# A two-block layer on one core: the depthwise convolution's work divided anew between VectorE, TensorE and an accumulating DMA

## The chip, the cores and the metric

The kernel runs on one core of a Trainium2 chip. The metric is the device time of one execution in microseconds (us), as the median of several runs.

## What is computed

The reference runs two model blocks on 256 tokens of width 1024, all in float32: a first block (a gated feed-forward, a token mixer with two kinds of attention, another feed-forward) and a second block (a Conformer convolution, a feed-forward, a gate, attention with forget gates, and so on). The change lies in the convolution of the second block:

```python
def conformer_conv(hn, w_pw1, b_pw1, w_dw, b_dw, ln_g, ln_b, w_pw2, b_pw2):
    u = hn @ w_pw1 + b_pw1
    a, g = jnp.split(u, 2, axis=-1)
    u = a * jax.nn.sigmoid(g)
    kern = w_dw[:, None, :].astype(u.dtype)
    u = lax.conv_general_dilated(
        u, kern, window_strides=(1,), padding=((CONV_WIDTH - 1, 0),),
        dimension_numbers=("NWC", "WIO", "NWC"),
        feature_group_count=D_MODEL) + b_dw
    u = layernorm(u, ln_g, ln_b)
    u = jax.nn.silu(u)
    return u @ w_pw2 + b_pw2
```

Each of the 1024 channels is filtered by its own 31 taps over the 256 tokens, causally. Before it stands a product with a 1024x2048 matrix, behind it a layer norm over the channels, which needs every channel.

## The kernel before

**The weight stream.** Activations lie transposed, 128 channels on the partitions and 256 tokens along the free dimension; 1024 channels are eight such tiles. All weights come as one stream of chunks of 128x1024 float32 (512 KB, eight 128x128 blocks). SP loads a chunk into a `raw` buffer (5 of them). ScalarE copies it into `hi`, rounded to fp32r (L239, 4 buffers), and VectorE writes the rest, raw minus hi, into `lo` (L243, 4 buffers). A product of a block with an activation, which is split in the same way, is then three fp32r matmuls (`mm3`, L260 to L262: hi with the activation's upper part, hi with its lower part, lo with its upper part).

**The convolution's stage** (`conv`, L1159). For each of the eight channel tiles n, `pw1(n)` makes two groups of 24 such matmuls, one for each half of the gate, from one chunk each, so the stage uses 16 chunks. VectorE multiplies each half by the row scale R (L1186, L1189), ScalarE adds biases and takes a tanh, VectorE joins both into `cu`, the padded input of the filter (L1193). ScalarE copies `cu` into `cx`, which holds even and odd tokens apart (L1199, four small copies).

`conv_out(n)` filters one tile. The 31 taps are divided: TensorE takes LAGS = 11 pairs of taps in each of two groups g of 64 channels, as float32 matmuls with diagonal matrices `cw` or `dw` (L1214; one float32 matmul is two rows of the trace). ScalarE brings the two results into `cb` (L1217). VectorE takes the other REST = 10 taps as shifted products, one instruction a tap, in two chains of five (tile `a` for even, tile `t` for odd taps): the first of a chain is a TENSOR_SCALAR (L1226), the others SCALAR_TENSOR_TENSORs that add to the chain (L1228). Then it adds the two chains (L1229), for n > 0 a `shift` (L1231), and in `stats` the TensorE part `cb` (L1236). The shift, tile `cm`, is tile 0's mean over its channels, negated, taken from the finished tile 0 by a matmul (L1240) and a copy (L1242); it goes to every tile so that the later variance is well behaved. `stats` also sums the tiles and their squares (L1250, L390) for the layer norm.

**What sets the order.** The program is written with tiles and pools, and a scheduler orders the instructions of each engine ahead of time, by its own estimate of when each can run. On the chip each engine then takes its instructions strictly in that order, and a waiting instruction holds up everything behind it on its engine.

```python
            for d in range(LAGS):
                nc.tensor.matmul(o, w[:, d], x[:, g, 16 - d : 16 + P - d], start=(d == 0), stop=(d == LAGS - 1))
```

Of the kernel before, what the change touches and what calls it, by code (L numbers as in the profile page):

```python
# [9 lines left out]
F32 = mybir.dt.float32  # L10
# [3 lines left out]
ALU = mybir.AluOpType  # L14
# [11 lines left out]
EPS = 1e-6  # L26
NEG = -1e30
TAPS = 31
LAGS = 11
AHEAD = 2  # L30
WARM = 10
WIDE = 6
# [84 lines left out]
class Kern:  # L117
# [104 lines left out]
    def prefetch(self, two=False):  # L222
# [17 lines left out]

        def low(i):
            s = slice(i * h, (i + 1) * h)
            nc.vector.tensor_tensor(lo[:, s], raw[:, s], hi[:, s].bitcast(F32), op=ALU.subtract)  # L243

        self.ready.append((chunk, hi, lo))
# [913 lines left out]
    def conv(self, X, R, after):  # L1159
# [44 lines left out]
        def conv_out(n, u, x):  # L1204
            b = self.bank("pt")
            back = self.p([P, T], "cb", 2)
            for g in range(2):
# [7 lines left out]
                for r in range(2):  # L1215
# [2 lines left out]
                        back[g * HD : g * HD + HD, r::2], o[h], AF.Identity, scale=0.5, bias=dwb[h, n, g : g + 1]  # L1218
                    )

            v = [self.a("u"), self.t("t")]
            for i in range(REST):
                w = v[i % 2]
                s, c = u[:, i : i + T], dww[:, n, i : i + 1]
                if i < 2:
                    nc.vector.tensor_scalar(w, s, c, None, op0=ALU.mult)  # L1226
                else:
                    nc.vector.scalar_tensor_tensor(w, s, c, w, op0=ALU.mult, op1=ALU.add)  # L1228
            nc.vector.tensor_tensor(v[0], v[0], v[1], op=ALU.add)  # L1229
            if n:  # L1230
                nc.vector.tensor_tensor(v[0], v[0], self.shift, op=ALU.add)  # L1231
            return v[0], back

        def stats(n, v, back):
            nonlocal acc, acc2
            nc.vector.tensor_tensor(v, v, back, op=ALU.add)  # L1236
            if n == 0:

                b = self.bank("pt")
                nc.tensor.matmul(b[:, :T], nmean, v, start=True, stop=True)  # L1240
                self.shift = self.p([P, T], "cm0", 1)
                nc.vector.tensor_copy(self.shift, b[:, :T])  # L1242
                v0 = v
                v = self.a("v")
                nc.vector.tensor_tensor(v, v0, self.shift, op=ALU.add)
                acc = self.t("acc")
                nc.vector.tensor_copy(acc, v)
            else:
                if n < KD - 1:
                    nc.vector.tensor_tensor(acc, acc, v, op=ALU.add)  # L1250
            acc2 = self.square_into(acc2, v, n == KD - 1)
            U.append(v)

        todo = []
        for n in range(KD):
            x = pw1(n)
            if n > 1:
                stats(n - 2, *todo.pop(0))
            if n:
                todo.append(conv_out(n - 1, *prev))  # L1260
            prev = x
        todo.append(conv_out(KD - 1, *prev))
        for n in (KD - 2, KD - 1):
            stats(n, *todo.pop(0))
        self.stage = "convLN"
        XP = [self.split(t) for t in self.ple_loads(0)]
        while len(self.ready) < PRE:
# [495 lines left out]
```

## Time and profile before

| | |
|---|---|
| median of three runs | 1367.5 us (1366.8, 1367.5, 1372.15) |
| profiled execution, its own time | 1364.68 us |
| its span | 1362.9 us |
| TensorE (PE) busy | 1337.7 us, 98% of the span |
| VectorE (DVE) busy | 1066.6 us, 78% |
| ScalarE (ACT) busy | 860.0 us, 63% |
| GpSimd (POOL) busy | 146.8 us, 11% |
| DMA | 234.11 MB, mean 172 GB/s |

The span is the profiler's stretch from the first to the last instruction; the execution's own time holds 1.8 us more around it. A busy share is an average over stages with different limits: what a change in one stage is worth is read from that stage, from the time of each engine in it and from the wait that ends last there. Matmuls overlap in the records, so what one costs is the distance between the starts of neighbours, not its duration. The same holds for neighbours on the other engines.

### The profile page before, as it was taken

The page shows a single profiled execution, that of the slowest core. Times are in us where ns is not written, and L with a number is a line of the kernel's source. Part 1 is how long each engine was busy: PE and PEld are TensorE (multiplying, and loading weights), DVE is VectorE, ACT ScalarE, POOL GpSimd, SP SyncE. Part 2 cuts the span into 40 slices and gives each one's busy share as a digit, 9 for nine tenths or more (in the row PEclk, how much of TensorE's full clock was granted, in tenths as well). Part 3 has the DMA queues.
Part 4 walks back from the last instruction along what each step waited for, and adds up shares of the span by engine and source line. Part 5 has one row for each costly group of instructions (what it writes and reads, how often), then busy time and mean ns, then how long its engine had stood idle before and what let it go on. Part 6 is the DMA issues. An engine that isn't in the chain of part 4 may idle for free. (4 is left out here: it accounts for less than half of the span.)

```text
span 1362.9 us, 25065 instructions
## 1 busy us (share of the span) xinstructions
PE 1337.7 (98%) x9111; PEld 1210.0 (89%) x9111; DVE 1066.6 (78%) x2381; ACT 860.0 (63%) x1994; POOL 146.8 (11%) x197
## 2 busy tenths in 40 slices
PE   8999999999999999999999999999999999999997
PEld 7888898899988998888899998888897989888887
DVE  7877668798887779987779798766678986976665
ACT  6666544678787556666655586654557785665554
POOL 0111000000000001310010003220001210431000
PEclk9999999999999999999999999999999999999999
DMA  8666665643332655666666145666655444666561
GB/s 281 186 186 186 189 190 201 232 128 121 110 109 84 193 175 185 189 198 186 193 220 226 73 139 183 194 194 188 189 168 163 140 124 140 202 189 193 189 188 45
DMA packets 65228, 234.11 MB, mean 172 GB/s; under 512 B 7536, under 2 KB 8208, under 8 KB 65104
## 3 DMA queue, kind: packets, MB, share of 16 engines
q1 hardware_dynamic: 63648, 230.89, 54.0%
q8 instruction: 72, 1.18, 0.3%
q10 hardware_dynamic: 1296, 1.35, 0.3%
q0 software_dynamic: 160, 0.26, 0.1%
q14 instruction: 52, 0.43, 0.1%
HBM read 231.43 MB, written 1.05 MB: 171 GB/s over the span
## 5 line engine op out<-in xcount | busy, mean ns | idle before, releaser
L239 ACT ACTIVATE hi<-raw 128x512 fp32r<-128x512 f32 (+1 forms) x759 | 471.9, 666 | 382.7 <-issue 187.8
L243 DVE TENSOR_TENSOR lo<-raw,hi 128x512 fp32r<-128x512 f32 (+1 forms) x759 | 542.9, 749 | 180.3 <-ACT hi L239 178.1
L260 PE MATMUL mm<-a,hi 128*128 128x256 f32 x654 | 194.2, 297 | 0.5 <-ACT a L1127 0.5
L262 PE MATMUL mm<-a,lo 128*128 128x256 f32 x654 | 185.0, 283 | 0.0
L261 PE MATMUL mm<-a,hi 128*128 128x256 f32 x654 | 184.9, 283 | 0.0
L271 PE MATMUL at<-a,hi 128*128 128x512 f32 x408 | 146.9, 398 | 2.3 <-DVE a L368 2.3
L271 PE MATMUL s<-a,hi 128*128 128x512 f32 x416 | 148.2, 394 | 0.0
L271 PE MATMUL mm<-a,hi 128*128 128x512 f32 x392 | 139.8, 394 | 0.0
L365 POOL TENSOR_TENSOR H<-t,H 128x256 fp32r<-128x256 f32 x108 | 105.9, 981 | 302.5 <-ACT H L364 298.3
L260 PEld LDWEIGHTS mm<-a,hi 128*128 128x128 f32 x654 | 125.2, 191 | 4.2 <-issue 2.7
L261 PEld LDWEIGHTS mm<-a,hi 128*128 128x128 f32 x654 | 125.2, 191 | 0.0
L262 PEld LDWEIGHTS mm<-a,lo 128*128 128x128 f32 x654 | 124.8, 191 | 0.0
L272 PE MATMUL s<-a,lo 128*128 128x256 f32 x416 | 116.5, 280 | 0.0
L272 PE MATMUL at<-a,lo 128*128 128x256 f32 x408 | 115.1, 282 | 0.5 <-DVE lo L243 0.5
L271 PE MATMUL at<-H,hi 128*128 128x512 f32 x324 | 113.0, 393 | 0.0
L272 PE MATMUL mm<-a,lo 128*128 128x256 f32 x392 | 109.8, 280 | 0.0
L271 PE MATMUL mm<-H,hi 128*128 128x512 f32 x292 | 102.0, 393 | 0.0
L271 PEld LDWEIGHTS at<-a,hi 128*128 128x128 f32 x408 | 77.1, 189 | 20.2 <-ACT hi L239 2.6
L271 PEld LDWEIGHTS s<-a,hi 128*128 128x128 f32 x416 | 78.0, 187 | 17.7
L272 PE MATMUL at<-H,lo 128*128 128x256 f32 x324 | 90.1, 278 | 0.0
L271 PEld LDWEIGHTS mm<-a,hi 128*128 128x128 f32 x392 | 73.5, 187 | 16.5
L271 PE MATMUL s<-H,hi 128*128 128x512 f32 x248 | 86.4, 393 | 0.0
(412 smaller groups left out, 2980.3 us busy)
## 6 DMA issues: line engine op xcount, KB each, us to landing
raw<-in_wts SPq DMA_DIRECT2D x423, 512.0 KB, 4.2
cw<-in_dwp SPq DMA_DIRECT2D x9, 704.0 KB, 4.6
x<-in_xT SPq DMA_DIRECT2D x4, 256.0 KB, 6.2
raw<-in_wts SPq DMA_DIRECT2D x2, 256.0 KB, 5.8
e<-in_pT ACTq DMA_DIRECT2D x4, 128.0 KB, 5.1
out_dram<-o ACTq DMA_DIRECT2D x2, 256.0 KB, 3.0
out_dram<-o SPq DMA_DIRECT2D x2, 256.0 KB, 3.1
cst<-in_cst SPq DMA_DIRECT2D x1, 416.0 KB, 8.2
```

The source lines that it names most:

```text
L239: nc.scalar.activation(hi[:, s], raw[:, s], AF.Copy)
L243: nc.vector.tensor_tensor(lo[:, s], raw[:, s], hi[:, s].bitcast(F32), op=ALU.subtract)
L260: nc.tensor.matmul(out, sh, mh, start=(first and i == 0), stop=False)
L261: nc.tensor.matmul(out, sh, ml, start=False, stop=False)
L262: nc.tensor.matmul(out, sl, mh, start=False, stop=(last and i == n - 1))
L271: nc.tensor.matmul(b, sh, m.rearrange("p i n -> p (i n)"), start=(k == 0), stop=False)
L272: nc.tensor.matmul(b[:, T:], sl, mh, start=False, stop=(k == len(X) - 1))
L365: (low or nc.vector).tensor_tensor(lo, src, hi.bitcast(F32), op=ALU.subtract)
```

## The change

Three things are done, all in the convolution's stage.

1. The 16 chunks that are loaded for `pw1` get their `lo` in another way. ScalarE writes `lo` = -`hi`, and a DMA issued by GpSimd then reads the chunk from HBM a second time and adds it to `lo` in place. VectorE's subtraction is gone for these chunks.
2. LAGS goes from 11 to 9, so REST goes from 10 to 14: TensorE loses two lags in each of the 16 groups, VectorE gains four taps in each of the eight tiles. The tables `cw` and `dw` shrink from 11 to 9 matrices.
3. Two additions are folded into the chains: the even chain begins with a SCALAR_TENSOR_TENSOR that adds `shift` (for n > 0), the odd chain with one that adds `cb`. The additions of L1231 and L1236 are gone.

```diff
-LAGS = 11
+LAGS = 9
@@ prefetch
         def low(i):
             s = slice(i * h, (i + 1) * h)
+            if self.stage == "conv":
+
+                nc.scalar.mul(lo[:, s], hi[:, s].bitcast(F32), -1.0)
+                nc.gpsimd.dma_start(lo[:, s], self.ap["wts"][chunk, :, s], accum_op=ALU.add)
+                return
             nc.vector.tensor_tensor(lo[:, s], raw[:, s], hi[:, s].bitcast(F32), op=ALU.subtract)
@@ conv_out
             v = [self.a("u"), self.t("t")]
+            base = [self.shift if n else None, back]
             for i in range(REST):
                 w = v[i % 2]
                 s, c = u[:, i : i + T], dww[:, n, i : i + 1]
-                if i < 2:
+                on = base[i] if i < 2 else w
+                if on is None:
                     nc.vector.tensor_scalar(w, s, c, None, op0=ALU.mult)
                 else:
-                    nc.vector.scalar_tensor_tensor(w, s, c, w, op0=ALU.mult, op1=ALU.add)
+                    nc.vector.scalar_tensor_tensor(w, s, c, on, op0=ALU.mult, op1=ALU.add)
             nc.vector.tensor_tensor(v[0], v[0], v[1], op=ALU.add)
-            if n:
-                nc.vector.tensor_tensor(v[0], v[0], self.shift, op=ALU.add)
-            return v[0], back
+            return v[0]
 
-        def stats(n, v, back):
+        def stats(n, v):
             nonlocal acc, acc2
-            nc.vector.tensor_tensor(v, v, back, op=ALU.add)
```

The new lines push the later line numbers up by five to seven. The scheduler makes a new order of everything in the stage. Three places of it matter here. The numbers in the names tell buffers apart.

**GpSimd's queue at the start of the stage, before.** `dww` and `dwb` are the tap weights of VectorE and the biases, `rs_y` are two reciprocal roots from which the row scale R is made:

```order
L1171 DMA dww_8781<-in_dww 128x80
L1174 DMA dwb_8784<-in_dwb 128x16
L1192 MEMSET cu_8856 128x30
L1196 MEMSET cx_8859 128x2x16
L1192 MEMSET cu_8933 128x30
L1196 MEMSET cx_8936 128x2x16
L1192 MEMSET cu_9055 128x30
L1192 MEMSET cu_9188 128x30
L407 TENSOR_TENSOR rs_y_8733<-rs_v_8731,mhalf 128x2
L407 TENSOR_TENSOR rs_y_8741<-rs_v_8739,mhalf 128x2
```

The same place now; `lo_8903` is the last of four accumulating loads that stand ahead, `lo_8996` the first of twelve that follow:

```order
L246 DMA lo_8903<-in_wts 128x1024
L1176 DMA dww_8781<-in_dww 128x112
L1179 DMA dwb_8784<-in_dwb 128x16
L1197 MEMSET cu_8858 128x30
L1201 MEMSET cx_8861 128x2x16
L1197 MEMSET cu_8937 128x30
L1201 MEMSET cx_8940 128x2x16
L1197 MEMSET cu_9061 128x30
L1197 MEMSET cu_9194 128x30
L412 TENSOR_TENSOR rs_y_8733<-rs_v_8731,mhalf 128x2
L412 TENSOR_TENSOR rs_y_8741<-rs_v_8739,mhalf 128x2
L246 DMA lo_8996<-in_wts 128x1024
```

So `dww` stands behind four accumulating loads, and the fifth such load stands behind both roots.

**TensorE at the fifth chunk of the stage, before** (`s`, `mm` and `at` are PSUM banks; `hi_8991` and `lo_8992` are the fifth chunk, `hi_9021` the sixth):

```order
L262 MATMUL s_8866<-a_8717,lo_8900 128x256
L260 MATMUL mm_8987<-a_8134,hi_8991 128x256
L261 MATMUL mm_8987<-a_8134,hi_8991 128x256
L260 MATMUL at_8988<-a_8134,hi_9021 128x256
L261 MATMUL at_8988<-a_8134,hi_9021 128x256
L262 MATMUL mm_8987<-a_8134,lo_8992 128x256
```

And now, where `hi_8995`, `hi_9026`, `hi_9128` and `hi_9159` are the fifth to the eighth chunk:

```order
L267 MATMUL s_8868<-a_8717,lo_8903 128x256
L265 MATMUL mm_8991<-a_8134,hi_8995 128x256
L266 MATMUL mm_8991<-a_8134,hi_8995 128x256
L265 MATMUL at_8992<-a_8134,hi_9026 128x256
L266 MATMUL at_8992<-a_8134,hi_9026 128x256
L265 MATMUL s_9124<-a_8134,hi_9128 128x256
L266 MATMUL s_9124<-a_8134,hi_9128 128x256
L265 MATMUL mm_9125<-a_8134,hi_9159 128x256
L266 MATMUL mm_9125<-a_8134,hi_9159 128x256
L267 MATMUL mm_8991<-a_8134,lo_8996 128x256
```

TensorE begins four chunks ahead, with the products that need `hi` alone, before the first that needs the fifth chunk's `lo`.

**VectorE at the end of the stage, before.** These are the last instructions ahead of the layer norm's column sums; `cb_9749` is the TensorE part of the last tile, n = 7, and `cb_9707` that of n = 6:

```order
L1229 TENSOR_TENSOR a_9734<-a_9734,t_9735 128x256
L390 TENSOR_TENSOR acc_9073<-acc_9073,sq_9580 128x256
L1229 TENSOR_TENSOR a_9734<-a_9734,t_9776 128x256
L1250 TENSOR_TENSOR acc_9071<-acc_9071,a_9487 128x256
L1231 TENSOR_TENSOR a_9734<-a_9734,cm_9067 128x256
L390 TENSOR_TENSOR acc_9073<-acc_9073,sq_9703 128x256
L1231 TENSOR_TENSOR a_9734<-a_9734,cm_9067 128x256
L1236 TENSOR_TENSOR a_9734<-a_9734,cb_9707 128x256
L1250 TENSOR_TENSOR acc_9071<-acc_9071,a_9734 128x256
L390 TENSOR_TENSOR acc_9073<-acc_9073,sq_9791 128x256
L1236 TENSOR_TENSOR a_9734<-a_9734,cb_9749 128x256
```

And now, from the instruction that takes the last tile's `cb` in, with `t_9736` and `t_9776` the odd chains of n = 6 and n = 7:

```order
L1236 SCALAR_TENSOR_TENSOR t_9776<-cu_9698,dww_8781,cb_9753 128x256
L395 TENSOR_TENSOR acc_9078<-acc_9078,sq_9708 128x256
L1236 SCALAR_TENSOR_TENSOR t_9736<-cu_9575,dww_8781,t_9736 128x256
L1236 SCALAR_TENSOR_TENSOR a_9735<-cu_9698,dww_8781,a_9735 128x256
L1236 SCALAR_TENSOR_TENSOR t_9776<-cu_9698,dww_8781,t_9776 128x256
L1236 SCALAR_TENSOR_TENSOR t_9736<-cu_9575,dww_8781,t_9736 128x256
L1236 SCALAR_TENSOR_TENSOR t_9776<-cu_9698,dww_8781,t_9776 128x256
L1236 SCALAR_TENSOR_TENSOR t_9736<-cu_9575,dww_8781,t_9736 128x256
L1236 SCALAR_TENSOR_TENSOR t_9776<-cu_9698,dww_8781,t_9776 128x256
L1237 TENSOR_TENSOR a_9735<-a_9735,t_9736 128x256
L1236 SCALAR_TENSOR_TENSOR t_9776<-cu_9698,dww_8781,t_9776 128x256
L1255 TENSOR_TENSOR acc_9076<-acc_9076,a_9735 128x256
```

Behind the last row shown stand two more steps of `t_9776`, a sum of squares and the joining addition. `cb` of a tile was the last thing that VectorE added; now it goes into the first of the odd chain's seven steps, and the other six and an addition follow it.

## Rows read from the trace of the kernel before

**Rows 1.** Windows view: busy us of each engine, TensorE clock, DMA share, GB/s
```profile
core 0: us, PE busy (x) PEld busy (x) DVE busy (x) ACT busy (x) POOL busy (x), PEclk, DMA share, GB/s
690.00:760.00 70.00, 68.93 (x586) 68.52 (x585) 62.19 (x152) 38.80 (x80) 4.89 (x18) 1.00 0.68 230
760.00:780.00 20.00, 20.00 (x180) 20.00 (x179) 15.19 (x43) 12.48 (x35) 0.25 (x2) 1.00 0.01 2
784.00:786.00 2.00, 2.00 (x11) 2.00 (x11) 1.15 (x7) 0.38 (x1) 0.69 (x1) 0.50 0.00 0
786.00:788.00 2.00, 2.00 (x14) 2.00 (x13) 1.04 (x3) 0.38 (x1) 0.00 (x0) 0.66 0.00 0
```
**Rows 2.** Timeline of TensorE: start, us, instruction, count, [idle before it, releaser]
```profile
691.30 0.28 PE L260 MATMUL mm<-a,hi 128*128 128x256 f32 x1
...
697.19 0.29 PE L261 MATMUL s<-a,hi 128*128 128x256 f32 x1
...
715.47 0.28 PE L261 MATMUL at<-a,hi 128*128 128x256 f32 x1
715.59 2.62 PE L1214 MATMUL pt<-cx,cw 128*128 128x128 f32 x22
717.96 0.36 PE L262 MATMUL at<-a,lo 128*128 128x256 f32 x1
...
756.10 5.18 PE L1214 MATMUL pt<-cx,cw 128*128 128x128 f32 x44 [1.07 <-ACT cb L1217]
...
780.47 0.28 PE L398 MATMUL pt<-ones,acc 128*128 128x1 f32 x2
```
**Rows 3.** Timeline of VectorE in the convolution's stage, the same columns
```profile
699.69 0.20 DVE L1172 TENSOR_SCALAR dww<-dww 128x80 f32<-128x80 f32 x1 [3.51 <-DMA dww<-in_dww]
...
704.41 2.35 DVE L243 TENSOR_TENSOR lo<-raw,hi 128x1024 fp32r<-128x1024 f32 x2
706.69 0.75 DVE L426 COPY R<-pt 128x256 f32<-128x256 f32 x2
...
708.68 2.76 DVE L1594 TENSOR_TENSOR a<-a,R 128x256 f32<-128x256 f32 x8
...
736.66 1.28 DVE L243 TENSOR_TENSOR lo<-raw,hi 128x512 fp32r<-128x512 f32 x2
...
743.39 1.13 DVE L1226 TENSOR_SCALAR a<-cu,dww 128x256 f32<-128x256 f32 x4
...
746.64 1.67 DVE L1228 SCALAR_TENSOR_TENSOR a<-cu,dww,a 128x256 f32<-128x256 f32 x4
...
758.45 0.75 DVE L1229 TENSOR_TENSOR a<-a,t 128x256 f32<-128x256 f32 x2
...
778.99 0.43 DVE L1236 TENSOR_TENSOR a<-a,cb 128x256 f32<-128x256 f32 x1 [3.47 <-ACT cb L1217]
...
781.45 0.42 DVE L1236 TENSOR_TENSOR a<-a,cb 128x256 f32<-128x256 f32 x1 [1.12 <-ACT cb L1217]
```
**Rows 4.** Timeline of ScalarE, the same columns
```profile
682.88 1.06 ACT L239 ACTIVATE hi<-raw 128x1024 fp32r<-128x1024 f32 x1 [1.44 <-PE at L271]
...
697.51 2.96 ACT L239 ACTIVATE hi<-raw 128x1024 fp32r<-128x1024 f32 x3 [3.81 <-PE s L261]
...
712.94 1.33 ACT L1199 ACTIVATE cx<-cu 64x128 f32<-64x128 f32 x4
```
**Rows 5.** Timeline of GpSimd, the same columns
```profile
692.59 0.58 POOL L1171 DMA_DIRECT2D dww<-in_dww  x1 [59.80 <-DVE nmean L1176]
...
700.71 1.64 POOL L407 TENSOR_TENSOR rs_y<-rs_v,mhalf 128x2 f32<-128x2 f32 x1 [3.73 <-DVE rs_v L412]
724.15 0.12 POOL L1196 MEMSET cx<- 128x32 f32 x1 [21.80 <-PE pt L1214]
```
**Rows 6.** DMA view, 640 to 800 us: issues, KB each, median us to landing
```profile
raw<-in_wts SPq DMA_DIRECT2D x37, 512.0 KB, 3.6
cw<-in_dwp SPq DMA_DIRECT2D x9, 704.0 KB, 4.6
dww<-in_dww POOLq DMA_DIRECT2D x1, 40.0 KB, 7.1
```

More of the change, by code (lines that the diff above doesn't have):

```diff
@@ L1257, in conv @@
             if n > 1:
-                stats(n - 2, *todo.pop(0))
+                stats(n - 2, todo.pop(0))
             if n:
@@ L1263, in conv @@
         for n in (KD - 2, KD - 1):
-            stats(n, *todo.pop(0))
+            stats(n, todo.pop(0))
         self.stage = "convLN"
```

## The prediction

> **What bounds the kernel now.** I read the windows first. From 690 to 760 us TensorE is busy for 68.93 of 70 us at full clock, VectorE for 62.19, and the DMA engines have a share of 0.68; from 760 to 780 TensorE is busy throughout and VectorE only for 15.19 [rows 1]. So TensorE sets the pace, with VectorE close behind, and both must be followed in order of time. The timeline of TensorE gives its prices by the distance of neighbours: a product costs 0.12 us (715.47 to 715.59), and a filter group of 22 rows 2.37 us (715.59 to 717.96), so 0.108 a row. It stands still once in the filter, for 1.07 us, waiting for ScalarE to empty a bank, and its filter ends at 780.47 [rows 2]. VectorE's last addition then waits for the last `cb` and ends at 781.45 + 0.42 = 781.87; only then come the layer norm's sums. VectorE's prices are read in the same way. One addition takes 0.42 and two 0.75, so 0.33 each; a chain step costs 0.40 (four in 1.67), a chain's first multiplication 0.26 (four in 1.13), a whole-chunk subtraction 1.13 (two in 2.35), a half-chunk one 0.60 (two in 1.28) [rows 3].
>
> **The change, counted alone.** TensorE loses two lags, so four rows, in each of 16 groups: 64 x 0.108 = 6.9 us. With the 1.07 us stall gone as well, 8.0 us is the most that TensorE can give back. VectorE goes from 64 to 111 chain steps (+47 x 0.40 = 18.8 us), from 16 first multiplications to one (-3.9), from 23 additions to eight (-5.0), and loses 16 subtractions (-18.1): net -8.2 us. ScalarE gains 16 negations, by the copies of a chunk (three in 2.96 us [rows 4]) about 0.96 each, 15 us in a stretch where it is busy for 38.80 of 70 us [rows 1]; that lies beside other work except where named below. The smaller tap tables of an earlier stage save VectorE work under a full TensorE; I count nothing.
>
> **VectorE becomes the bound, by its order.** Each chain for n > 0 now begins with the shift, which needs the finished tile 0. So I place the shift's copy. In the new order the instruction that stands at 697.19 in the trace [rows 2] has six products fewer ahead of it: 696.5. From there 35 products (4.2 us), four float32 broadcasts (eight rows, 0.9 us) and 14 products (1.7 us) lead to 703.3, where TensorE wants the eighth chunk's `hi`. ScalarE can start refilling at about 696.9 and has seven chunk operations up to that `hi`, 6.7 us: 703.6. Two products later, at 704.0, TensorE wants the fifth chunk's `lo`. After 22 more products it comes to the first filter group at 706.6, but `cx` is not there. R no longer stands behind the 3.51 us wait for `dww` and the subtractions that delay it to 706.69 [rows 3]; it is copied by 702.6. Behind it VectorE has three products with R (1.0), the eight multiplications of x (2.76 in the trace) and two operations for `cu`: 707.0. The four copies into `cx` take 1.33 us [rows 4]: 708.3. Then two groups of 18 rows (1.9 us each), 96 products (11.5 us) and the mean's matmul (0.4) lead to 724.1, and VectorE copies the shift at 724.3.
>
> Behind that copy the order lists 102 chain steps, 29 additions and the like, two copies and eight half-chunk subtractions: 40.8 + 9.6 + 0.7 + 4.8 = 55.9 us. VectorE would end at 780.2 instead of 781.87: **-1.7 us**. TensorE's filter ends at about 772.5 (780.47 less 8.0), but that time isn't on the path. By the same counts each later `cb` arrives within a microsecond before VectorE takes it, so a delay of TensorE passes on in full. The waits for `cb` at the end (3.47 and 1.12 us [rows 3]) are not a gain beyond this: VectorE now has chain steps there.
>
> **The accumulating loads.** No row shows one, so I bound its time L from issue to landing. The lower end is a chunk's plain load from SP, 3.6 us; the upper is the slow small load of GpSimd's queue in this very stage, 7.1 us for 40 KB, and 3.6 us on top, 10.7 [rows 6]. I take 7.0, because `dww` is the nearest row in queue and time. What L may be free of charge: the second chunk's `hi` is written from 682.88 to 683.9 [rows 4], two small operations and the negation follow, and the load can go at 685.7; TensorE wants the result two products after 691.30 [rows 2], so at 691.5: 5.8 us. The fifth chunk's negation ends at 699.8 (three operations after 696.9), `lo` is wanted at 704.0, and the 1.7 us wait for `cx` would come anyway: 5.9 us. A late second chunk also delays the refill of the fifth, so the two add up: 2 x (7.0 - 5.8) = **+2.4 us**, with 0 at the lower end and 9.8 at the upper. Later chunks have about 7 us or more.
>
> The Trainium skill's page "DMA: Bandwidth & Descriptors" (section "Anatomy of one DMA - SWDGE (gpsimd) path") fits 2.0 us plus bytes over 436 GB/s to such a load: 3.2 us for a chunk, as an estimate. By it the 2.4 us would be 0. The trace speaks against it under load: the same formula gives `dww` 2.1 us, and it took 7.1 [rows 6].
>
> GpSimd's queue: the two roots now stand behind four loads, which go by 691, five microseconds before the roots can start; the fifth load stands behind the second root, whose row took 1.64 us [rows 5] and is through by 699. `dww` goes behind four loads too; VectorE reads it just before it copies R, so it may take up to 10 us. Loads now also queue behind the `cx` fills, which wait for TensorE (21.80 us in one case [rows 5]); the first such load needs its negation at about the same time, the others are wanted 10 us later. Issuing costs about 0.58 us each [rows 5], beside other work. None of this is added.
>
> **TensorE's clock.** After the waits at 780 the granted clock was 0.50 from 784 to 786 and 0.66 in the next window [rows 1]. Now TensorE has nothing to do from about 772.5 until the column sums, so the low level comes earlier. These sums are 16 rows, 1.7 us; at half clock they cost 1.7 more, at full clock nothing; I take **+0.8**.
>
> **Sum.** -1.7 + 2.4 + 0.8 = +1.5 us. The profiled execution of 1364.68 us (span 1362.9 and 1.8 around it) would become 1366.2. It lies 2.8 us under the median of the runs, so against 1367.5 I forecast **1369.0 us**: the same, where a measurement of this kernel tells about 0.5%, 6.8 us, from no change.
>
> **Rivals.** *The loads land in time.* With L under 5.8 us the sum is -1.7 + 0.8 = -0.9: 1366.6 us. For it speaks 3.6 us of SP's load, against it `dww`. Chance 0.19; also "the same".
>
> *The DMA engines become the bound, slower.* Between 690 and 760 us they move 230 GB/s at a share of 0.68 [rows 1], so 338 GB/s when full, and 16.1 MB in all. The smaller `cw` tables take 1.2 MB away (nine loads of 704 KB [rows 6] become 576), which leaves 14.9 MB or 44.1 us. Twelve accumulating loads fall in this stretch, and 25.9 us are left for them, 2.16 us of all engines each; as plain loads of 0.52 MB they would need 1.55. It decides when an accumulating load occupies the engines for more than 1.4 times a plain one. At twice, 12 x 3.1 = 37.2 us, the supply of chunks ends 11.3 us late: -1.7 + 0.8 + 11.3 = +10.4, 1377.9 us. Against it speaks that some weight loads of the next stage can move into the stretch from 760 to 780, where the share is 0.01 [rows 1]. The Trainium skill's page "Collectives: The Full Stack" (section "The bandwidth ceiling: the fold count and why AG ≠ RS ≠ AR") says that an add inside a DMA reads two sources and so moves half as much as a copy. By that rule this rival would hold; no run here shows it yet. Chance 0.27.
>
> *TensorE's relief counts in full, faster.* -8.0 us: 1359.5 us. VectorE's 55.9 us would have to start by 718.0, while TensorE's own order puts the shift at 722 even with no wait at all. Chance 0.06.
>
> **How the numbers follow.** My forecast, with L between 5.8 and about 9 us, has 0.48; with the first rival 0.67 lies within 0.5%; slower by over 0.5% (above 1374.3 us) has 0.27, from the DMA rival and L near its upper end (-1.7 + 9.8 + 0.8 = +8.9); faster (below 1360.7) has 0.06. The range goes from 1363.5, below the first rival by the scatter of runs and part of the way to the fast case, to 1381, above the DMA rival by a few microseconds.
>
> **What would show it.** Right: VectorE without a gap from about 724 to 780, TensorE idle before the column sums, short TensorE waits for `lo` at the second and fifth chunk, landings of about 7 us. Wrong: a shift copy far from 724; waits for `lo` in the later chunks and a DMA share near 1.0 (the DMA rival); VectorE waiting for `cb` at the end, so that TensorE still sets it (the fast case); VectorE waiting for `dww`.

## The result, and the profile after

The changed kernel takes 1385.74 us as the median of four runs (1382.37 to 1387.86), beside 1368.28 for the kernel before on the same chip: a ratio of 1.0118, 95% interval 1.010 to 1.0135. It is 1.2% slower, clear of the noise; the forecast was 1369.0, and the range ended at 1381. The profiled execution took 1382.37 us with a span of 1380.6.

The time is lost in one place. I count **the stage** from VectorE's `bgh` (the first line of `conv`) to its first operation `r` on the layer norm's sums. Before, that is 692.11 to 783.69, 91.6 us; after, 691.72 to 800.86, 109.1: 17.5 us more. What follows `r` takes 579.2 us before and 579.7 after. Since the start of the stage scatters by some 6 us among the runs below (691.5 to 697.9), the stage compares them better than their medians do; it is that of one execution of each kernel. The kernel `probe` below is the kernel before up to the end of the stage, and its stage takes 91.3 us beside 91.6. One help for reading the rows after: the chain steps of L1228 stand at L1236 now, and the joining addition of L1229 at L1237.

The windows after, to be read against [rows 1]:

```profile
core 0: us, PE busy (x) PEld busy (x) DVE busy (x) ACT busy (x) POOL busy (x), PEclk, DMA share, GB/s
690.00:760.00 70.00, 59.99 (x471) 58.70 (x472) 42.46 (x117) 46.20 (x85) 15.07 (x30) 0.95 1.04 295
760.00:780.00 20.00, 20.00 (x162) 20.00 (x161) 16.14 (x40) 10.87 (x26) 0.37 (x3) 0.91 0.29 86
690.00:700.00 10.00, 7.71 (x51) 7.62 (x51) 2.37 (x9) 2.78 (x6) 2.39 (x9) 0.83 1.06 275
700.00:708.00 8.00, 6.63 (x43) 6.63 (x44) 1.91 (x10) 4.37 (x5) 2.50 (x4) 0.79 0.97 338
...
760.00:764.00 4.00, 4.00 (x24) 4.00 (x23) 1.50 (x5) 0.75 (x2) 0.00 (x0) 0.59 0.41 82
```

The DMA engines, at 0.68 before, are full from 690 to 760 (the view's share can come out a little over 1). TensorE, which worked through that stretch before, now stands still for 10.0 of 70 us, and the granted clock is under 1.00 in three places, where before it was 1.00 throughout. VectorE is busy for 42.46 us instead of 62.19; that by itself says little, since twelve whole-chunk subtractions that stood there (13.6 us) are gone; its waits are read from its timeline below.

What was late, by the DMA issues from 690 to 760 (engine, count, size, median us from issue to landing; [rows 6] has them for a longer stretch):

```profile
raw<-in_wts SPq DMA_DIRECT2D x13, 512.0 KB, 10.9
lo<-in_wts POOLq DMA_DIRECT2D x13, 512.0 KB, 10.0
cw<-in_dwp SPq DMA_DIRECT2D x9, 576.0 KB, 11.3
```

In the same stretch before, `raw` took 4.4 us and `cw` 4.6. It is not only the new loads that are slow: the plain loads of chunks and tables beside them take more than twice as long. Over all 16 accumulating loads the median is 9.9 us, and the longest 14.2.

TensorE's waits, in its timeline (start, duration, instruction, idle time before and what ended it; [rows 2] is its timeline before):

```profile
692.03 0.39 PE L267 MATMUL s<-a,lo 128*128 128x256 f32 x1 [2.50 <-DMA lo<-in_wts]
...
701.37 0.38 PE L267 MATMUL at<-a,lo 128*128 128x256 f32 x1 [1.63 <-DMA lo<-in_wts]
...
714.03 0.39 PE L267 MATMUL mm<-a,lo 128*128 128x256 f32 x1 [1.83 <-DMA lo<-in_wts]
...
747.83 4.26 PE L1219 MATMUL pt<-cx,cw 128*128 128x128 f32 x36 [2.07 <-ACT lo L245]
759.62 3.17 PE L1219 MATMUL pt<-cx,cw 128*128 128x128 f32 x18 [1.83 <-DMA cw<-in_dwp]
...
796.19 0.56 PE L403 MATMUL pt<-ones,acc 128*128 128x1 f32 x2 [5.67 <-DVE acc L1255]
```

Three chunks' `lo` and two `cw` tables come late. The loads behind the first three waits are the first, the third and the fifth that were issued: at 683.15, 689.09 and 706.88, landing after 8.8, 12.2 and 7.1 us. The 2.07 us before 747.83 are put down to a negation that this filter does not read; a `cw` table that was issued at 735.51 landed 12.2 us later, at 747.69, just before the filter began, so it was most likely this table that ended the wait. Behind three of these waits, those that end at 692.03, 701.37 and 759.62, TensorE ran at the lower of its two clock levels (1.2 GHz) for some microseconds (a granted clock of 0.50 from 693 to 695, 703 to 706 and 761 to 764): these are the windows above with 0.83, 0.79 and 0.59. Behind the other two, of 1.83 and 2.07 us, the clock stayed at 1.00. VectorE's timeline, against [rows 3]:

```profile
691.72 0.28 DVE L1169 TENSOR_SCALAR bgh<-cols 128x8 f32<-128x8 f32 x1
...
709.31 0.87 DVE L431 COPY R<-pt 128x256 f32<-128x256 f32 x2 [2.86 <-PE pt L427]
...
733.51 0.42 DVE L1247 COPY cm<-pt 128x256 f32<-128x256 f32 x1 [0.73 <-PE pt L1245]
...
750.90 0.48 DVE L1236 SCALAR_TENSOR_TENSOR t<-cu,dww,cb 128x256 f32<-128x256 f32 x1 [2.24 <-ACT cb L1222]
...
764.55 0.42 DVE L1194 TENSOR_TENSOR th<-s,R 128x256 f32<-128x256 f32 x1 [3.06 <-PE s L267]
...
797.20 0.42 DVE L1237 TENSOR_TENSOR a<-a,t 128x256 f32<-128x256 f32 x1
...
800.86 0.16 DVE L1318 TENSOR_SCALAR r<-pt 128x2 f32<-128x2 f32 x1 [3.23 <-PE pt L403]
```

ScalarE's next refills of `hi`, which began at 697.51 [rows 4], begin at 703.63. The shift is copied at 733.51, not at 724.3, and behind it VectorE waits for `cb` and for TensorE's products, which it did not do in the forecast.

### The profile page after: what moved, and what is told of

The parts are those of the page before. It is cut to its first block, busy times and chain, and to the rows that moved or that the text cites. A ratio compares the mean times of both kernels' runs of the same rounds, so it can differ in the third digit from the quotient of the medians.

```text
span 1380.6 us, 24980 instructions
## 1 busy us (share of the span) xinstructions
PE 1338.7 (97%) x9047; PEld 1210.0 (88%) x9047; DVE 1059.1 (77%) x2382; ACT 874.9 (63%) x2010; POOL 156.4 (11%) x213
## 3 DMA queue, kind: packets, MB, share of 16 engines
q1 hardware_dynamic: 63648, 229.71, 48.8%
## 5 line engine op out<-in xcount | busy, mean ns | idle before, releaser
L248 DVE TENSOR_TENSOR lo<-raw,hi 128x512 fp32r<-128x512 f32 (+1 forms) x743 | 523.2, 739 | 177.1 <-ACT hi L239 174.9
L370 POOL TENSOR_TENSOR H<-t,H 128x256 fp32r<-128x256 f32 x108 | 102.5, 950 | 305.8 <-ACT H L369 301.6
## 6 DMA issues: line engine op xcount, KB each, us to landing
cw<-in_dwp SPq DMA_DIRECT2D x9, 576.0 KB, 11.3
```

The source lines that it names most:

```text
L370: (low or nc.vector).tensor_tensor(lo, src, hi.bitcast(F32), op=ALU.subtract)
```

## The experiments

The theory that I took to the chip: the accumulating loads occupy the DMA engines far longer than plain ones, everything lands late, and TensorE waits (T1). Its rivals: the chain hi, negation, issue, landing is slow whatever the load does (T2); the new division of taps and the order on VectorE cost it (T3). All runs in one table. A ratio compares a kernel with the kernel before as it ran beside it on the same chip (medians of 1367.3 to 1370.5 us), so it isn't the quotient of two medians of this table. The last three columns are of the profiled execution (`lo`: median us to landing of GpSimd's loads; probe has one execution):

| kernel | median us | ratio to before (95%) | stage us | bgh to shift | `lo` |
|---|---|---|---|---|---|
| before | 1368.28 | | 91.6 | 48.8 | |
| the change | 1385.74 | 1.0118 (1.010 to 1.0135) | 109.1 | 41.8 | 9.9 |
| plain_load | 1374.27 | 1.0024 (1.0011 to 1.0037) | 95.6 | 34.4 | 5.5 |
| vector_low | 1376.15 | 1.0058 (1.0036 to 1.008) | 99.1 | 42.3 | |
| dma_low_alone | 1379.83 | 1.007 (1.0055 to 1.0085) | 104.5 | 37.0 | 9.1 |
| folds_alone | 1371.05 | 1.0024 (1.0011 to 1.0038) | 94.9 | 41.4 | |
| folds_not_last | 1369.24 | 1.0007 (0.999 to 1.0024) | 90.7 | 41.3 | |
| sbuf_source | 1384.11 | 1.011 (1.0079 to 1.0141) | 107.5 | 41.1 | 9.1 |
| pool_low | 1387.51 | 1.0136 (1.0109 to 1.0164) | 108.0 | 46.4 | |
| pool_low_late_shift | 1389.21 | 1.0144 (1.0119 to 1.017) | 109.1 | 48.3 | |
| pool_half_dma | 1379.2 | 1.0077 (1.0049 to 1.0105) | 101.1 | 40.4 | 6.3 |
| half_dma | 1379.28 | 1.0082 (1.0051 to 1.0113) | 100.9 | 41.5 | 8.4 |
| mix9 | 1376.58 | 1.006 (1.0038 to 1.0083) | 99.0 | 42.2 | 8.4 |
| mix10 | 1376.0 | 1.0051 (1.0031 to 1.0071) | 96.5 | 44.7 | 8.3 |
| lags10_tail | 1370.49 | 1.0012 (0.9997 to 1.0026) | 93.0 | 42.2 | |
| late_dma | 1384.42 | 1.0109 (1.009 to 1.0129) | 109.4 | 43.6 | 9.8 |
| late_shift | 1386.4 | 1.0121 (1.0098 to 1.0144) | 107.9 | 41.6 | 9.9 |
| one_table | 1383.0 | 1.0122 (1.0103 to 1.014) | 106.2 | 47.2 | 9.3 |
| probe | 1366.19 | | 91.3 | 48.4 | |

### The add alone: plain_load

```diff
-                nc.gpsimd.dma_start(lo[:, s], self.ap["wts"][chunk, :, s], accum_op=ALU.add)
+                nc.gpsimd.dma_start(lo[:, s], self.ap["wts"][chunk, :, s])
```

> The change, but GpSimd's 16 loads into `lo` write instead of add, so the output lacks the subtraction; the negation, the queue, the bytes read from HBM and the order stay. T1 (an accumulating load costs the DMA engines nearly twice a plain one; the engines are full from 690 to 760 and everything lands late): the DMA share between 690 and 760 falls to about 0.85, the loads land in about 5 us, the wait of TensorE at the stage's beginning goes, and the time is 1367 to 1373 us. T2 (the latency of the chain hi, negation, issue, landing on GpSimd's queue, whatever the load does): as the change, 1381 to 1387 us, landings near 10 us. T3 (the new split of taps and VectorE's order): 1381 to 1387 us, with landings that are short.

The instructions stand in the same order on all five engines as in the change, so nothing but the add differs. The stage takes 95.6 us instead of 109.1: **the add costs 13.5 us**, and T2 and T3 fall as the main cause. The ratios, 1.0024 and 1.0118, say nearly the same (0.94% are 13 us). T1's own numbers were a little too good: the median is 1.3 us over its range, the share 0.91 instead of 0.85. Windows, DMA issues from 690 to 760, all waits of TensorE for a load, and the marks of the stage:

```profile
690.00:760.00 70.00, 67.34 (x557) 66.13 (x557) 47.81 (x129) 54.22 (x99) 11.89 (x32) 1.00 0.91 317
```
```profile
raw<-in_wts SPq DMA_DIRECT2D x16, 512.0 KB, 4.9
lo<-in_wts POOLq DMA_DIRECT2D x15, 512.0 KB, 5.6
cw<-in_dwp SPq DMA_DIRECT2D x9, 576.0 KB, 7.4
```
```profile
702.60 0.39 PE L267 MATMUL at<-a,lo 128*128 128x256 f32 x1 [1.24 <-DMA lo<-in_wts]
...
713.11 0.39 PE L267 MATMUL mm<-a,lo 128*128 128x256 f32 x1 [1.15 <-DMA lo<-in_wts]
```
```profile
697.61 0.23 DVE L1169 TENSOR_SCALAR bgh<-cols 128x8 f32<-128x8 f32 x1
...
732.00 0.42 DVE L1247 COPY cm<-pt 128x256 f32<-128x256 f32 x1 [0.72 <-PE pt L1245]
...
793.23 0.16 DVE L1318 TENSOR_SCALAR r<-pt 128x2 f32<-128x2 f32 x1 [3.24 <-PE pt L403]
```

In the whole stage the loads into `lo` move as many bytes as in the change, and in this window more is moved per second (317 instead of 295 GB/s), at a lower share. TensorE stands still for 2.7 us in these 70 instead of 10.0, and its clock stays at 1.00. That makes 7.3 us of waits, and at half clock the change lost 10 x 0.17 + 8 x 0.21 + 4 x 0.41 = 5.0 us in the three windows shown above: 12.3 of the 13.5 us. VectorE's timeline shows the same loss from its side: the 7.4 us by which the shift comes sooner (34.4 instead of 41.8 behind `bgh`) are the first half of it; VectorE's waits from the shift to its last addition, 7.7 us in the change and 1.7 here, the second.

### The price of one load: probe

```diff
+        probe = self.p([P, CH * P], "probe", 1)
+        nc.scalar.activation(probe[:, :T], U[-1], AF.Copy)
+        nc.gpsimd.dma_start(probe, self.ap["wts"][0])
+        nc.gpsimd.dma_start(probe, self.ap["wts"][1], accum_op=ALU.add)
...
```

> The kernel before, with four more loads on GpSimd's queue into one unused tile of 128x1024 after the last `stats` (a plain one, an accumulating one, and the two again); nothing reads the tile, and the computation is that of before. Each waits for the one before, in a stretch where the DMA engines have a share near 0. Theory (the add occupies the engines 2.7 us instead of 1.6): plain 3.3 to 3.8 us from issue to landing, accumulating 4.4 to 5.5. Rival (an accumulating load is only slow among other traffic): both 3.3 to 3.8.

The first two loads, in GpSimd's timeline and in the windows that hold each of them alone:

```profile
784.33 0.58 POOL L1268 DMA_DIRECT2D probe<-in_wts  x1 [11.85 <-ACT probe L1267]
...
788.57 0.93 POOL L1269 DMA_DIRECT2D probe<-in_wts  x1 [2.05 <-DMA probe<-in_wts]
```
```profile
784.00:789.00 5.00, 5.00 (x32) 5.00 (x32) 1.89 (x10) 0.81 (x3) 1.72 (x3) 0.66 0.35 105
789.00:794.30 5.30, 4.28 (x36) 4.07 (x35) 5.16 (x15) 4.45 (x11) 0.50 (x1) 1.00 0.61 99
```

Both windows move one chunk (105 GB/s x 5.00 us and 99 x 5.30 are 0.525 MB). The plain load lands 3.9 us after its issue and occupies all engines for 0.35 x 5.00 = 1.75 us; the accumulating one lands after 5.5 us and occupies them for 0.61 x 5.30 = 3.2, **1.85 times as long**. The plain landing is a little above the theory's range, the other at its upper end. The third, a plain one, took 3.9 us again; the fourth, an accumulating one among the next stage's traffic, took 8.1 us. So the add is slow by itself, and slower still where the engines are crowded.

The Trainium skill's page "Collectives: The Full Stack" (section "The bandwidth ceiling: the fold count and why AG ≠ RS ≠ AR") says of a collective that its reduce moves half as much as its copy, because the add needs two source reads. It does not speak of a kernel's own load; the 1.85 here comes near its two.

### Not the second read of HBM: sbuf_source

```diff
-                nc.gpsimd.dma_start(lo[:, s], self.ap["wts"][chunk, :, s], accum_op=ALU.add)
+                nc.gpsimd.dma_start(lo[:, s], raw[:, s], accum_op=ALU.add)
```

> The change with the accumulating load reading the chunk from the raw buffer in SBUF instead of from HBM a second time; all else as changed. T1 (the add itself occupies the engines longer, whatever its source): stage 105 to 112 us, time 1380 to 1386 us, landings 9 us or more, GpSimd's queue near 24% of the engines' time between 640 and 820. Rival (the second read from HBM is what costs): the queue's share falls to about 14%, landings to 6 us, stage 95 to 99 us.

107.5 us and 9.1 us to landing, as T1 has it. The queue's line between 640 and 820 (packets, MB, share of the engines' time) is that of the change, which has 24.1% there; with plain loads it was 14.4%. In these 180 us that is 2.7 us of all engines for each of the 16 accumulating loads, and 1.6 for each plain one.

```profile
q0 software_dynamic: 2368, 8.46, 24.4%
```

### The loads without the rest: dma_low_alone

```diff
+            if self.stage == "conv":
+                nc.scalar.mul(lo[:, s], hi[:, s].bitcast(F32), -1.0)
+                nc.gpsimd.dma_start(lo[:, s], self.ap["wts"][chunk, :, s], accum_op=ALU.add)
+                return
```

> The kernel before with the 16 accumulating loads alone: 11 lags, 10 shifts, no addition folded in. The `cw` tables are 704 KB again, so the DMA engines have 1.2 MB more to move than under the change. T1: 1384 to 1392 us, DMA share 1.0 from 690 to 765. T2: 1378 to 1385 us. T3: 1364 to 1369 us, since VectorE only loses work.

104.5 us, 12.9 more than before: three quarters of the 17.5 come with the loads alone. (The ratio gives less, 1.007, which is 9.6 us beside the change's 16.) The time is under T1's 1384 to 1392 and inside T2's 1378 to 1385, so this run by itself doesn't tell the two apart; plain_load does. But this kernel shows best how the loss comes about. Its two disturbed windows, and TensorE's waits in them:

```profile
690.00:700.00 10.00, 7.21 (x36) 7.01 (x36) 2.21 (x8) 3.47 (x7) 3.02 (x10) 0.66 1.05 269
...
710.00:720.00 10.00, 6.64 (x33) 6.22 (x32) 9.96 (x29) 6.33 (x16) 1.73 (x2) 0.66 1.04 256
```
```profile
693.02 0.58 PE L267 MATMUL s<-a,lo 128*128 128x256 f32 x1 [2.79 <-DMA lo<-in_wts]
...
714.42 5.06 PE L1219 MATMUL pt<-cx,cw 128*128 128x128 f32 x22 [3.10 <-ACT cx L1204]
```

TensorE bounds this kernel, and it stood still for 2.79 + 3.36 = 6.2 us in these windows; at a mean clock of 0.66 it lost 2 x 10 x 0.34 = 6.8 more, less some 0.7 because the clock fell before the waits had ended (0.62 from 713 to 714, while TensorE stood still until 714.42). Together 12.3, beside the 12.9 measured. Two late arrivals (2.8 us for a `lo`, 3.1 for a `cx` that was late in its turn) cost twice their length, because the half clock followed each.

### Taps and folds: vector_low, folds_alone, folds_not_last

vector_low is the change with its new branch in `prefetch` taken out; folds_alone is that with 11 lags; folds_not_last is folds_alone with the last tile's `cb` added at the end:

```diff
-            base = [self.shift if n else None, back]
+            base = [self.shift if n > 0 else None, back if n < KD - 1 else None]
...
             nc.vector.tensor_tensor(v[0], v[0], v[1], op=ALU.add)
+            if base[1] is None:
+                nc.vector.tensor_tensor(v[0], v[0], back, op=ALU.add)
```

> The change without its accumulating loads: VectorE subtracts again, the taps stay at 9 lags and 14 shifts, both additions stay folded in. VectorE gets 18.1 us back on top of -8.2, so +9.9 us in a stage where it waited for 6.7 us before 700 and 4.6 us after 770: it ends 3 to 6 us later than before. T1 and T2: 1371 to 1375 us, with a DMA share near 0.7 and no wait of TensorE for `lo` or `cw`. T3: 1381 to 1387 us.

> The kernel before with the two additions folded into the chains alone: 11 lags, 10 shifts, VectorE subtracts. VectorE loses 5.0 us of additions and pays 2.1 us for 15 chain steps in place of multiplications; each chain for n > 0 now waits for the shift. T1 and T2: 1365 to 1370 us. T3 (the shift at the head of the chains holds VectorE up): 1373 us or more.

> The kernel with the folds alone (11 lags, VectorE subtracts, stage 94.9 us), but the last tile's `cb` is added at the end instead of at the head of its chain. If the folds cost 3.3 us because the last `cb` has the whole odd chain behind it (five steps of 0.40 and an addition, 2.3 us, where before one addition stood): stage 92 to 93.5 us. Rival (the shift at the head of the chains costs it): stage 94.5 to 96 us.

vector_low came out 7.5 us over before, a little above what T1 and T2 had for its median, with VectorE at work nearly throughout and TensorE free 10.5 us before the column sums. The folds alone cost 3.3 us in the stage although they save VectorE work; their median, 1371.05, lies between the two ranges. Their last rows say why they cost, first folds_alone, then folds_not_last:

```profile
783.28 0.48 DVE L1231 SCALAR_TENSOR_TENSOR t<-cu,dww,cb 128x256 f32<-128x256 f32 x1 [0.58 <-ACT cb L1217]
783.80 2.05 DVE L1231 SCALAR_TENSOR_TENSOR t<-cu,dww,t 128x256 f32<-128x256 f32 x4
785.89 0.42 DVE L1232 TENSOR_TENSOR a<-a,t 128x256 f32<-128x256 f32 x1
789.53 0.16 DVE L1313 TENSOR_SCALAR r<-pt 128x2 f32<-128x2 f32 x1 [3.22 <-PE pt L398]
```
```profile
786.35 0.42 DVE L1236 TENSOR_TENSOR a<-a,cb 128x256 f32<-128x256 f32 x1
786.68 0.42 DVE L390 TENSOR_TENSOR acc<-acc,sq 128x256 f32<-128x256 f32 x1
788.58 0.16 DVE L1317 TENSOR_SCALAR r<-pt 128x2 f32<-128x2 f32 x1 [1.48 <-PE pt L398]
```

In the first the last `cb` has a whole chain and an addition behind it, and the sums come 6.25 us after it, 3.22 of them a wait for a TensorE that had stood idle; in the second one addition follows, and the sums come after 2.23. With that the stage is 90.7 us, better than the 92 to 93.5 expected and 0.9 better than before; in the median it is the same as before.

### Other places for the subtraction: pool_low, pool_low_late_shift, pool_half_dma

```diff
-                nc.scalar.mul(lo[:, s], hi[:, s].bitcast(F32), -1.0)
-                nc.gpsimd.dma_start(lo[:, s], self.ap["wts"][chunk, :, s], accum_op=ALU.add)
+                nc.gpsimd.tensor_tensor(lo[:, s], raw[:, s], hi[:, s].bitcast(F32), op=ALU.subtract)
```

pool_low_late_shift also adds the shift at each tile's end instead of at the head of its chain (`base = [None, back]`); pool_half_dma is the change with GpSimd's subtraction for every second chunk and the accumulating load for the others.

> The change with GpSimd subtracting (raw minus hi) in place of the negation and the accumulating load; 9 lags, 14 shifts, both folds. The stage is counted from VectorE's `bgh` to its first operation on the layer norm's sums: 91.6 us before, 109.1 changed, 95.6 with plain loads. GpSimd takes 0.98 us for 128x256 elsewhere in the program, so 3.9 for a chunk and 62 us in all, beside other work. T1 (the adds in the DMA engines cost the 13.5 us): stage 94 to 97 us, time 1368 to 1372 us. Rival: GpSimd's work slows VectorE's instructions down, so that the chain steps come at 0.44 us or more instead of 0.40: stage 98 to 102 us.

> As the kernel with GpSimd's subtractions, but only the addition of `cb` is folded into a chain; the shift is added at the end again, so that no chain waits for the first tile. VectorE has 1.4 us more work. If the place of the shift at the head of seven chains is what holds VectorE: stage 87 to 92 us, time 1362 to 1367 us, the best of the kernels so far. Rival (VectorE is held by its work, not by the shift): stage 95 to 98 us.

> Eight chunks by the accumulating load, the eight between them by GpSimd's subtraction; 9 lags, both folds. T1 (it costs because the engines are full: 12 loads at 2.7 us of all 16 engines in a stretch that has 25.9 us left): eight loads at most need 21.6 us, so the engines have room, landings fall to 5 to 7 us and the stage is within 2 us of that with GpSimd alone (94 to 98 us). Rival (every accumulating load costs time by itself): half of the 13.5 us stays, stage 101 to 104 us, landings of 9 us or more.

All three missed the theory's ranges. pool_low (108.0) and pool_low_late_shift (109.1) lie above their rivals' ranges too; pool_half_dma (101.1) lies in its rival's, but with short landings. What pool_low's rival had in mind, GpSimd slowing VectorE down, is there by far. VectorE's and GpSimd's timelines of pool_low:

```profile
716.51 2.30 DVE L1197 SCALAR_TENSOR_TENSOR cu<-u,th 128x256 f32<-128x256 f32 x1
...
719.44 0.42 DVE L1197 SCALAR_TENSOR_TENSOR cu<-u,th 128x256 f32<-128x256 f32 x1
...
723.43 2.33 DVE L1197 SCALAR_TENSOR_TENSOR cu<-u,th 128x256 f32<-128x256 f32 x1 [0.89 <-ACT u L1191]
```
```profile
716.09 2.42 POOL L245 TENSOR_TENSOR lo<-raw,hi 128x1024 fp32r<-128x1024 f32 x1 [0.79 <-ACT hi L239]
723.07 4.92 POOL L245 TENSOR_TENSOR lo<-raw,hi 128x1024 fp32r<-128x1024 f32 x2 [4.56 <-PE s L266]
```

An instruction of VectorE with two inputs in SBUF that starts during such a subtraction ends just after it: 2.30 and 2.33 us instead of 0.42. The subtractions moved to GpSimd take 2.6 us each, 41.7 in all, and each of the 16 holds up one instruction of VectorE: over the whole run VectorE is busy for 1086.9 us instead of the change's 1059.1, with the same number of instructions. In two places it is GpSimd that waits: the subtraction takes 3.55 and 3.75 us, and VectorE's chain steps at its start keep their 0.47. The Trainium skill's page "SBUF — State Buffer" (section "Who interferes with whom") states this: the two engines share a pair of ports, which is locked for a whole instruction. The trace agrees. So neither the place of the shift nor the room on the engines could be judged from these runs; only that the eight accumulating loads of pool_half_dma landed after 6.3 us.

### Fewer loads: half_dma, mix9, mix10, lags10_tail, late_dma

```diff
             if self.stage == "conv":
+                self.seen = getattr(self, "seen", -1) + 1
+            if self.stage == "conv" and self.seen % 2:
```

That is half_dma. mix9 has `self.seen % 2 and self.seen > 2`, mix10 `self.seen % 4 == 3` with LAGS = 10, late_dma `self.seen > 3`; mix9, mix10 and lags10_tail (LAGS = 10, no accumulating load) also add the last `cb` and the second tile's shift at the end.

> The change with every second chunk of the stage (the second, fourth, ...) by the accumulating load and the others subtracted by VectorE; 9 lags, both folds. VectorE has 9 us less to do than with VectorE alone (stage 99.1 us). T1 (the cost comes from engines that are full: eight loads at 2.7 us of all engines need 21.6 us where 25.9 are left): landings 5 to 7 us, DMA share in 690 to 760 about 0.9, stage 91 to 95 us. Rival (each accumulating load costs time of its own, 13.5/16 each): 6.7 us above what VectorE alone would leave, stage 98 to 102 us.

> Seven chunks (the fourth, sixth, ... sixteenth) by the accumulating load, nine by VectorE, so none of the first three; 9 lags. `cb` is folded into the chain for the first seven tiles and added at the end for the last; the shift is folded for the tiles from the third on. VectorE's work is about what it was before, TensorE's 6.9 us less. If full engines and the chain behind the last `cb` were what cost: stage 87 to 91 us, time 1363 to 1367 us, a little faster than before. Rival (VectorE's work sets the end as soon as TensorE has less): stage 92 to 95 us.

> Four accumulating loads (the fourth, eighth, twelfth and sixteenth chunk), twelve subtractions by VectorE, 10 lags; `cb` folded for the first seven tiles, the shift from the third on. Without the four loads the stage took 93.0 us, with VectorE at work from 700 to 780; four subtractions less are 4.5 us. If four loads find room: stage 88 to 91 us, the best so far but for the measurement's 0.5%. Rival (each such load makes TensorE wait): stage 93 to 97 us.

> No accumulating load at all; 10 lags and 12 shifts; `cb` folded for the first seven tiles, the shift from the third on. TensorE has 3.5 us less than before, VectorE 6.4 for the taps less 2.4 for the folds, so 4 us more, against 4.6 us in which it waited for the last `cb` before. Expected: stage 89 to 92 us, time 1365 to 1369 us. Rival (VectorE sets the end): 94 to 97 us.

> The change with the first four chunks of the stage subtracted by VectorE, which is idle there, and the other twelve by the accumulating load. Theory (the waits of 2.5 and 1.6 us at the second and the fourth chunk and the half clock behind them are the first four loads' doing): TensorE does not wait before 700, stage 100 to 104 us. Rival (the twelve loads behind 700 fill the engines, and that alone sets the end): stage 106 to 110 us.

Here the theory missed its numbers, and the rivals' ranges held for half_dma (100.9), mix10 (96.5) and late_dma (109.4); mix9 (99.0) lies above both of its ranges. With eight loads instead of none the stage grew from 99.1 (vector_low) to 100.9, though VectorE had 9 us less to do, and with four from 93.0 (lags10_tail) to 96.5. Two things can be read. The loads of half_dma, mix9 and mix10 still land after 8.3 to 8.4 us, though the engines' share from 690 to 760 fell to 0.90, 0.86 and 0.77; and each of these kernels has two waits for a `lo`, the first near 703. mix10's window, its first wait, and its first two accumulating loads, issued at 692.35 and 709.83:

```profile
690.00:760.00 70.00, 65.79 (x543) 64.98 (x542) 51.36 (x124) 40.51 (x80) 7.38 (x21) 0.98 0.77 233
```
```profile
703.11 0.39 PE L269 MATMUL s<-a,lo 128*128 128x256 f32 x1 [2.62 <-DMA lo<-in_wts]
```
```profile
lo<-in_wts POOLq DMA_DIRECT2D x1, 512.0 KB, 10.7
lo<-in_wts POOLq DMA_DIRECT2D x1, 512.0 KB, 5.6
```

The clock in the window from 700 to 710 is 0.83. The first of the two loads was issued within 1.4 us of three `cw` tables and four smaller loads, and needed 10.7 us; the second had one plain load of a chunk beside it, and needed about what the probe's took alone, 5.5. The three tables landed after 9.8 to 12.3 us there, and after 6.7 to 9.4 at the same place of lags10_tail, which has no such load. So what else is on the engines in those few microseconds counts for more than the number of such loads in the stretch; that is read from these landings, and no run varies it alone. And in half_dma VectorE was spared work ahead of the shift, where it then stood idle; the work behind the shift stayed, so 59.4 us lie between shift and `r` where vector_low has 56.7. Leaving the first four chunks to VectorE (late_dma) only moved the loss: a wait of 5.96 us that ends at 713 in place of the first two, and again 109 us. (Those two waits end with the landings of the first and the third load, so they stand at the first and third chunk and not at the second and fourth, as I had it.) lags10_tail, without any such load, missed its 89 to 92 by a microsecond; VectorE was at 9.1 of 10 us or more from 700 to 780.

### What passes the delay on: late_shift, one_table

late_shift is the change with `base = [None, back]` and the shift added at the end; one_table loads `cw` once:

```diff
-                w = self.dwm.get((n, g))
+                w = self.dwm.get((n, g), getattr(self, "one", None))
                 if w is None:
-                    w = self.p([P, LAGS, P], "cw", NCW)
+                    w = self.one = self.p([P, LAGS, P], "cw", 1)
```

> The change with all 16 accumulating loads, but the shift is added at the end of each tile, not at the head of its chain. Theory (VectorE stands idle until the shift comes, and a late TensorE passes on through it): VectorE fills its gaps before 733 with chain steps, stage 102 to 106 us. Rival (VectorE waits for `cu` and `cb`, so TensorE's lateness passes on anyway): stage 107 to 111 us.

> The change with all 16 accumulating loads, but `cw` is loaded once instead of nine times and used for all nine groups, so the filter of eight groups has the wrong taps; the count of matmuls is unchanged. 4.7 MB of some 24 MB leave the stretch. Theory (full engines): the DMA share in 700 to 760 falls to about 0.85, landings of the accumulating loads to 6 to 8 us, `raw` loads to 5 us, stage 96 to 101 us instead of 109.1. Rival (each accumulating load is late by itself): stage 105 to 109 us.

Without the gate of the shift the stage took 107.9 us, as the rival had it: VectorE waits for `cb` and for products of TensorE instead. In one_table the order of instructions changed too, and the shift came 5.4 us later than in the change; behind it the loss is gone (59.0 us to `r` instead of 67.3; 61.2 with plain loads). Its 106.2 lie in the rival's range, since the waits before 723 stayed (2.6, 1.6, 1.5 and 2.3 us). The share fell only to 0.94 and the landings to 9.3 us, not to the theory's 0.85 and 6 to 8. How much of the loss a stretch with more room would give back stays open.

## Why the prediction was wrong

- **VectorE's order** was right. Behind the shift I counted 55.9 us of work; there are 64.1 less 7.7 of waits, 56.4, and with plain loads 58.0 less 1.7, 56.3. The shift was forecast 32.2 us behind `bgh`; with plain loads it came after 34.4. `dww` took 14.0 us where I had up to 10 free, and VectorE waited 1.08 us for it; it then waited 2.86 us for TensorE before it could copy R.
- **The accumulating loads** were the step that failed. I took 7.0 us to landing, between 3.6 and 10.7; the median was 9.9 and the longest 14.2, beyond my upper end. Worse than the size was the way of counting: a latency that is free up to 5.8 us, at two places, so 2 x 1.2. The first wait, 2.5 us, came at the first chunk, for which I had counted nothing: its load went at 683.15, TensorE stood ready for it 6.4 us later, and it landed after 8.8. At the fifth chunk the landing was as forecast, 7.1 us, but the load went at 706.88 and not at 699.8, because the late TensorE held ScalarE's refill. There were more places (the third chunk and two `cw` tables), `raw` and `cw` became late with the loads (4.4 to 10.9 and 4.6 to 11.3 us), and half clock came behind three of the waits. The term of +2.4 was 13.5. The estimate of 3.2 us, which I had set beside it, lies below even the probe's landings with nothing beside them, 3.9 plain and 5.5 with the add.
- **The DMA rival** named the mechanism, with 0.27. It turned at 1.4 times a plain load; the probe has 1.85. Its price, 11.3 us late at twice, was near the 13.5, for a partly different reason: it counted the supply of chunks at the end of the stretch, while waits and half clock already began at 692. By its count over the whole stretch eight loads would have fitted, and those of half_dma still came late. The range reached that rival's 1377.9 and a few microseconds more; 13.5 instead of 11.3 and the next point took it beyond.
- **Without the loads' price** my sum was -0.9; with plain loads the stage is 4.0 us longer than before. Of these 4.9 us, 2.2 are the later shift, 2.1 lie between the shift's start and the end of VectorE's last addition (58.0 us instead of 55.9), 0.6 are the wait for the sums. So even with adds as cheap as plain loads the forecast would have been some 5 us too low, and its sign wrong.
- **The folds at the end** I had as no gain and no loss. folds_alone and folds_not_last show that a `cb` at the head of the last chain can cost. In the change VectorE waits only 0.29 us for the last `cb` and works on to the end, so how much of the loss is due to it isn't shown.
- **The clock** was right in kind and too small: TensorE was idle before the column sums (5.67 us), and `r` waited 3.23 us instead of 1.81, 1.4 where I took 0.8. The half clock inside the stage, about 5 us, I did not have.

No version beat the kernel before by what can be measured; folds_not_last and lags10_tail are level with it.

## What to carry to other kernels

A transfer that does arithmetic must be priced by how long it occupies the engines, against the room that the stretch has, before its latency is asked for: at a share of 0.68 there was room for plain loads but not for adds at 1.85 times the price. The room must be looked for in the few microseconds around each load and not in the mean of the stretch: at a mean of 0.77 one of four such loads landed after 10.7 us and TensorE waited for it. Where the engine that sets the pace waits, look for half clock behind the wait: in dma_low_alone it doubled the loss, while in the change it came behind three of the five waits. And before an addition is folded into the head of a chain, look at what arrives last: the whole chain then stands behind it.

## What the runs showed of the hardware that I had not expected

- A load that adds took 5.5 us alone where a plain one took 3.9 (512 KB), held the engines 3.2 us instead of 1.75, and was no quicker with its source in SBUF (9.1 us in the stage, 9.9 from HBM).
- GpSimd needs 0.86 and 0.93 us to issue it, 0.55 and 0.58 for a plain one.
- Its landing depends on what is beside it: in mix10 5.6 us beside one plain load, 10.7 beside three `cw` tables and four smaller loads.
- A subtraction on GpSimd stops VectorE's instructions with two inputs in SBUF until it ends (2.30 us instead of 0.42).
- In dma_low_alone, TensorE's waits of 2.8 and 3.1 us were each followed by so much half clock that the window of 10 us had a mean of 0.66. In the change a wait of 1.63 us was followed by it, others of 1.83 and 2.07 us were not.
